# Six small edits around the first output projection: a norm in other banks, the rotation's sum on GpSimd, splits and pair sums of the last head, casts and a lora norm

## The chip, the cores and the metric

The kernel runs on one core of a Trainium2 chip. Its engines are TensorE (PE, matrix products; PEld is its weight load), VectorE (DVE), ScalarE (ACT), GpSimd (POOL) and SyncE (SP), which issues every DMA. The metric is the device time of one launch in microseconds (us), the median of several runs. Times of the trace count from the start of the profiled span.

## The reference

Two encoder layers over 1024 tokens of width 1024, in float32. With `mod` from a conditioning vector `c`, each layer computes

```python
h = rmsnorm(x, norm_g) * (1 + scale) + shift
y = mixer(h)                       # layer 0: differential attention, layer 1: latent attention
x = x + gate * y                   # and a last rmsnorm after layer 1
```

Layer 0 projects `h` to queries, keys, values and a gate `z`, rotates queries and keys (rope), and has eight heads, each with two score maps of head size 64: `p = softmax(s1) - lam * softmax(s2)`, `o = p @ v`, an rmsnorm of `o` per head, `o * silu(z)`, and the output projection `o @ w_out0`. Layer 1 projects to a query latent of 384 and a key/value latent of 256 columns, each with an rmsnorm, expands them per head, and ends with `(o * silu(z)) @ w_out1`.

## The kernel before

**Split products.** A float32 product is computed by three matmuls of a rounded format: each operand is split into a high part (an ACT cast, `S.copy`) and a low part (raw minus high, on DVE or GpSimd), and `mm3` (lines 181 to 184) sums high x high, high x low and low x high in a PSUM bank. An operand is ready when its load has landed, ACT has cast it and the subtraction is done.

**Order.** The code is traced in program order, and a planner then orders each engine's instructions by its own estimate of when they are ready. Every engine, and SP's queue of DMA issues, runs its instructions strictly in that order. The code pins the order in places: `in_turn` (193) and `tc.keep_in_program_order` put an instruction behind the one traced before it on its engine, `tc.issue_after(ins)` and `behind("S")`, `behind("V")` (189) behind a given one, here the newest marked instruction of ACT or DVE. `mk.clear()` ends that in the projection. `side` is a queue of small jobs, of which each step of the projections' stream (`Stream.step`, 305) and each attention tile takes one: a tick.

**Heads of layer 0.** `attn0` (1002) takes a head in eight tiles of 128 queries. A tile (`q_tile`, 834) has two score maps in PSUM (L844, four matmuls each), of each the maximum on DVE (L397) and the exponential on ACT (L399), and the combined `e` on DVE (L852). `transpose_p` (375) transposes `e` through the only `tr` bank (L380), ACT casts it to `pth` (L382), DVE makes `ptl` (L383), and `pv` multiplies by the values. Between these, PE takes steps of the next head's projections. When half a strip of keys or queries is done, `rope` (312) copies it to `rp_raw` on ACT, four DMAs swap its rows into `rp_sw`, GpSimd multiplies by cosines (L324) and, three ticks later, by sines (L329); DVE adds the two (L333) in the job that stands seven ticks after the copy, and that job also stacks the result: two ACT casts (L341, L349), two GpSimd subtractions (L343, L351) and, for queries, four DMAs (L354, L355). Head 0 uses DVE for the cosines.

**The last head.** No projections are left for it. `extra0(i)` (1259) is called after each tile i = 0 to 7, and at three points of `run_tails` as 8, 9, 10. It fetches operands of the output projection (`fa`, `fw`), splits them (`both`), and takes `PRE0[i]` steps of `Pre7` (1201), each one `mm3` of products 0 and 1.

**The output projection** computes the 2 x 2 blocks of `o @ w_out` by seven products of four head pairs each (`Seven`, 1134; `fetch`, `split_a`, `split_w`, `mm`). Sums of heads (`combine`, 1115) are GpSimd operations. The last half head is still unfinished then: `tail0` sums its squares (`ssq`, L922), `tail_b` spreads the reciprocal norm over the partitions with four small products (`finish`, 876; L899, L900, `rb`) and scales `o` (L901); four DVE operations (L1332 to L1335) make its sums, which the third product needs as its fourth operand. PSUM has four `y` and two `tr` banks here; `ssq`, `rb` and half of the second product (`oz`) share the two `tr` banks, and `Y[0]`, `Y[1]` are unused until the third product. Products are added to `x` by `add0` (L1376); a kept part of the first product by `add_p1` (L1373) on GpSimd.

**Layer 1's start.** `group0` normalizes four row tiles (`norm_x`, 446, L454 on DVE or L452 on ACT) and transposes them (`h_chunk`, L465) while the seventh product runs; the first weight strips are loaded and split there (`strip1`, L227, L228). `lora` (1601) sums the squares of the latents over two or three strips on DVE (L1615), and sums that over partitions by four one-column products (L1620), at the step `NORM_AT` of the next half strip.

## Time and profile before

| what | value |
|---|---|
| runs | 1428.61, 1430.06, 1431.25 us; median 1430.06 |
| the profiled execution | 1430.7 us, of which the span of instructions is 1428.9 |
| PE, PEld | 1380.7 and 1149.6 us busy |
| DVE, ACT, POOL | 970.2, 737.0 and 720.0 us busy |
| DMA | 231.52 MB, mean 162 GB/s |
| mean granted clock of PE | 0.990 |

The heads of layer 0 run from about 148 to 704 us, its output projection to about 787, layer 1 from there. In rows of groups, the columns are line, engine, operation, output<-inputs, shape, count, then busy time in us and mean duration in ns, then the idle time of the engine before them and what ended it. In rows of a timeline: start and duration in us, line, operation, count of merged records; in square brackets the idle time before it and what ended that. A float32 matmul of 128 or one column leaves two records.

### The profile page before, as it was taken

The numbers are of one execution on the slowest core, as the hardware profiler recorded it, in microseconds if no ns is written. First come the engines' busy times: TensorE is split into PE (matmuls) and PEld (weight loads), VectorE is DVE, ScalarE is ACT, GpSimd is POOL, SyncE is SP. The second block draws the span as 40 slices with busy tenths as digits, with TensorE's granted clock in tenths as the row PEclk, the third lists the DMA queues.
The fourth block names the chain that finished last, engine by engine and source line by source line (L and its number), as shares of the span: only waits on it lengthen the run. The fifth ranks groups of instructions, "written<-read, shape, count | busy, mean of one in ns | idle before, by whom it ended". The sixth has DMA issues, their size and how long they took to land. (4 is left out here: it accounts for less than half of the span.)

```text
span 1428.9 us, 20757 instructions
## 1 busy us (share of the span) xinstructions
PE 1380.7 (97%) x7318; PEld 1149.6 (80%) x7318; DVE 970.2 (68%) x1383; ACT 737.0 (52%) x1325; POOL 720.0 (50%) x561
## 2 busy tenths in 40 slices
PE   8999999999999999999889999999999999999997
PEld 6777788888878788887767887787888888888886
DVE  8665778877777778677587876545666555555685
ACT  5523465656565556566536543335454454555554
POOL 5425264648585767564784233642131255653783
PEclk9999999999999999999999999999999999999999
DMA  9786634343443444424654136389444355566363
GB/s 345 245 243 196 191 103 131 89 143 104 147 141 113 136 127 121 148 79 166 206 185 155 45 90 215 121 283 257 145 132 119 103 165 190 180 212 210 132 252 118
DMA packets 149065, 231.52 MB, mean 162 GB/s; under 512 B 20577, under 2 KB 57569, under 8 KB 148962
## 3 DMA queue, kind: packets, MB, share of 16 engines
q1 hardware_dynamic: 148962, 230.21, 51.3%
q8 instruction: 57, 0.93, 0.3%
q14 instruction: 46, 0.38, 0.1%
HBM read 144.74 MB, written 61.81 MB: 145 GB/s over the span
## 5 line engine op out<-in xcount | busy, mean ns | idle before, releaser
L382 ACT CAST pth<-tr 128x512 fp32r<-128x512 f32 x256 | 150.4, 588 | 275.9 <-PE tr L380 272.2
L397 DVE TENSOR_REDUCE nm<-s 128x1 f32<-128x1024 f32 x192 | 233.7, 1218 | 67.2 <-PE s L844 55.3
L383 DVE TENSOR_TENSOR ptl<-tr,pth 128x512 fp32r<-128x512 f32 x256 | 176.0, 688 | 137.4 <-ACT pth L382 136.7
L228 POOL TENSOR_TENSOR wl<-wraw,wh 128x512 fp32r<-128x512 f32 (+2 forms) x79 | 104.7, 1327 | 203.8 <-ACT wh L227 190.7
L399 ACT ACTIVATE e<-s,nm 128x1024 f32<-128x1024 f32 x128 | 143.7, 1123 | 35.4 <-DVE nm L397 31.8
L380 PE MATMUL tr<-ident,e 128*128 128x128 f32 x1024 | 155.5, 274 | 5.4 <-DVE ptl L383 4.4
L380 PEld LDWEIGHTS tr<-ident,e 128*128 128x128 f32 x1024 | 120.2, 140 | 48.9 <-DVE ptl L383 25.1
L182 PE MATMUL acc<-h0h,wh 128*128 128x512 f32 x360 | 150.3, 418 | 1.8 <-DVE sl_w L926 0.9
L182 PE MATMUL pv<-pth,vt 128*128 128x256 f32 x512 | 147.4, 288 | 0.7 <-ACT pth L382 0.7
L183 PE MATMUL pv<-ptl,vt 128*128 128x256 f32 x512 | 145.8, 285 | 0.0
L184 PE MATMUL pv<-pth,vt 128*128 128x256 f32 x512 | 144.5, 282 | 0.0
L184 PE MATMUL acc<-h0h,wl 128*128 128x512 f32 x360 | 143.1, 397 | 0.6 <-POOL wl L228 0.6
L183 PE MATMUL acc<-h0l,wh 128*128 128x512 f32 x360 | 141.9, 394 | 0.0
L182 PEld LDWEIGHTS pv<-pth,vt 128*128 128x128 f32 x512 | 97.4, 190 | 3.7 <-ACT pth L382 0.9
L183 PEld LDWEIGHTS pv<-ptl,vt 128*128 128x128 f32 x512 | 97.6, 191 | 2.9
L184 PEld LDWEIGHTS pv<-pth,vt 128*128 128x128 f32 x512 | 97.6, 191 | 0.1
L324 POOL TENSOR_TENSOR rp_r<-rp_raw,cosT 128x512 f32<-128x512 f32 x38 | 50.2, 1322 | 93.0 <-ACT rp_raw L321 37.9
L329 POOL TENSOR_TENSOR rp_sw<-rp_sw,sinT 128x512 f32<-128x512 f32 x42 | 56.8, 1351 | 71.1 <-DMA rp_sw<-rp_raw 71.0
L1167 POOL TENSOR_TENSOR wol<-wol,woh 128x512 fp32r<-128x512 f32 x56 | 82.0, 1489 | 20.5 <-ACT woh L1166 20.5
L844 PE MATMUL s<-ks,qa 128*128 128x512 f32 x256 | 82.9, 405 | 4.3 <-DVE e L852 2.4
L852 DVE SCALAR_TENSOR_TENSOR e<-s,z,e 128x1024 f32<-128x1024 f32 x64 | 82.1, 1283 | 2.1
L184 PEld LDWEIGHTS acc<-h0h,wl 128*128 128x128 f32 x360 | 67.6, 188 | 16.3 <-POOL wl L228 1.1
(406 smaller groups left out, 3491.8 us busy)
## 6 DMA issues: line engine op xcount, KB each, us to landing
ada<-in_ada_ss SPq DMA_DIRECT2D x32, 512.0 KB, 5.4
wraw<-in_w_s SPq DMA_DIRECT2D x64, 256.0 KB, 2.8
vS<-v_hl SPq DMA_DIRECT2D x32, 512.0 KB, 6.0
vt<-vS SPq DMA_DIRECT2D x32, 512.0 KB, 4.1
wol<-tS SPq DMA_DIRECT2D x56, 256.0 KB, 4.8
tS<-ob SPq DMA_DIRECT2D x48, 256.0 KB, 2.0
rp_sw<-rp_raw SPq DMA_DIRECT2D x168, 64.0 KB, 2.0
bc_s<-bc_d SPq DMA_DIRECT2D x34, 256.0 KB, 3.9
```

The source lines that it names most:

```text
L182: PE.matmul(psum, ah, bh, start=first, stop=False, skip_group_check=skip)
L183: PE.matmul(psum, ah, bl, start=False, stop=False, skip_group_check=skip)
L184: mm3.last = PE.matmul(psum, al, bh, start=False, stop=last, skip_group_check=skip).ins
L228: sub = (V if pair_of else G).tensor_sub(l_[:, :n], raw[:, :n], f32v(h_[:, :n]))
L380: PE.transpose(tr[:, j, :], p[:, kt * P : (kt + 1) * P], ident)
L382: mk["S"] = S.copy(pth[kh][:, :, dst], tr).ins
L383: mk["V"] = V.tensor_sub(ptl[kh][:, :, dst], tr, f32v(pth[kh][:, :, dst])).ins
L397: mk["V"] = V.reduce_max(nm, s_ps, axis=AX.X, negate=True).ins
L399: mk["S"] = S.activation(e, s_ps, AF.Exp, bias=nm, scale=1.0, accum_out=zs).ins
L844: PE.matmul(s_ps[:, kc * HF : (kc + 1) * HF], src[:, c, ql], KS[h][kc][:, c, :], start=fst, stop=not fst)
L852: combined.append(V.scalar_tensor_tensor(out=e0, in0=e1, scalar=z1[:, 0:1], in1=e0, op0=ALU.mult, op1=ALU.add).ins)
L1167: sub = eng.tensor_sub(lo, raw, f32v(hi))
```

## The change

- **Norm in free banks.** `ssq` and `rb` of the last half head go to `Y[0]` and `Y[1]`; the four `L899` products go from DVE to ACT.
- **Rotation.** For heads 1 to 7 of layer 0 GpSimd adds right behind its product with the sines; the stack follows two ticks later than before.
- **Last head.** The splits stand one or two steps earlier, the loads of product 1 and of the last pair too, and the pair's sums (`combine`) move from the tail to steps 8 and 9. `PRE0` is spread anew. Layer 0's operand loads, while the heads run, keep their program order on SP, and the steps of `Pre7` stand behind the newest transpose on PE.
- **Kept product.** `add_p1` stands behind the newest GpSimd split.
- **Layer 1's start.** Two of the first group's four row tiles are scaled on ACT; the casts of the first two strips move behind, from one point of the sixth and seventh product to a later one.
- **Lora.** The last strip's square isn't added on DVE: the norm's one-column products sum two tiles instead. `NORM_AT` is 5.

```diff
 V1_AT = (3, 2)
-NORM_AT = 4
-PRE0 = (0, 0, 0, 0, 1, 1, 2, 2, 2, 3, 3)
+NORM_AT = 5
+PRE0 = (0, 0, 0, 0, 1, 2, 2, 2, 2, 2, 3)
 PRE1 = (0, 0, 0, 0, 0, 0, 0, 1, 1, 1, 1)
...
-    def rope(rp, acc, half, scale, eng=G):
+    def rope(rp, acc, half, scale, eng=G, add=V):
...
             in_turn(G.tensor_mul(sw, sw, sinT[:, cs]))
+            if add is G:
+                in_turn(G.tensor_add(r, r, sw))
...
         def fin():
-            with behind("V"):
-                V.tensor_add(r, r, sw)
+            if add is not G:
+                with behind("V"):
+                    V.tensor_add(r, r, sw)
             return r
...
             kt = kh * 4 + j
-            PE.transpose(tr[:, j, :], p[:, kt * P : (kt + 1) * P], ident)
+            transpose_p.last = PE.transpose(tr[:, j, :], p[:, kt * P : (kt + 1) * P], ident).ins
         dst = slice(t * P, (t + 1) * P)
...
         def f(acc, half):
-            rot, fin = rope(wp, acc, half, 1.0, G if h else V)
+            rot, fin = rope(wp, acc, half, 1.0, *[G if h else V] * 2)
...
                 t = a0a.tile([P, 2, HF], F32R, name="ks", tag="ks", bufs=4)
-                stack_k(t, fin())
+                stack_k(t, r.pop() if r else fin())
                 KS.setdefault(h, [None, None])[half] = t
...
-            side.add(*[None] * ROT, rot, *[None] * (DEF - 1 - ROT), g)
+            r = []
+            sum_ = [lambda: r.append(fin()), None] if h else []
+            side.add(*[None] * ROT, rot, *[None] * (DEF - 1 - ROT), *sum_, g)
         return f
...
         def f(acc, half):
-            rot, fin = rope(wp, acc, half, SC0, G if h else V)
+            rot, fin = rope(wp, acc, half, SC0, *[G if h else V] * 2)
...
                 qb = a0a.tile([P, 2, HF], F32R, name="qb", tag="qs", bufs=4)
-                stack_q(qa, qb, fin())
+                stack_q(qa, qb, r.pop() if r else fin())
                 QS.setdefault(h, [None, None])[half] = qa, qb
...
-            side.add(*[None] * ROT, rot, *[None] * (DEF - 1 - ROT), g)
+            r = []
+            sum_ = [lambda: r.append(fin()), None] if h else []
+            side.add(*[None] * ROT, rot, *[None] * (DEF - 1 - ROT), *sum_, g)
         return f
...
             return
-        rb = bank("z" if l else "tr", "rb", [P, HF])
+        rb = bank("z", "rb") if l else Y[1]
         for j in range(4):
             js = slice(j * P, (j + 1) * P)
-            if l:
-                S.mul(dgs[:, js], ident, y[:, j : j + 1])
-            else:
-                V.tensor_scalar(dgs[:, js], ident, y[:, j : j + 1], None, op0=ALU.mult)
+            S.mul(dgs[:, js], ident, y[:, j : j + 1])
             PE.matmul(rb[:, js], ones, dgs[:, js], start=True, stop=True)
...
-    ssq_at = []
+    ssq_at, Y = [], []
...
         def rest():
-            pt = bank("tr", "ssq", [P, HF]) if dst is not None else ssq_at[0] if ssq_at else bank("acc", "ssq")
+            pt = Y[0] if dst is not None else ssq_at[0] if ssq_at else bank("acc", "ssq")
             for j in range(4):
...
         def load(self, home, src):
-            self.last = SP.dma_start(f32v(home[1]), src).ins
+            ins = SP.dma_start(f32v(home[1]), src)
+            self.last = ins.ins
+            if mk and not self.l:
+                tc.keep_in_program_order(ins)
             return *home, f32v(home[1])
...
                 in_turn(sub)
+                self.sub = sub.ins
...
                 ssq_at.append(self.accs[1])
-            self.sv.mm(n, self.accs[i], h, i, start=True)
+            with tc.issue_after(transpose_p.last):
+                self.sv.mm(n, self.accs[i], h, i, start=True)
             self.n += 1
...
             fw(0, 3)
-            SP.dma_start(k0["11"], oF[0][3, 0])
-        if 3 <= i <= 6:
-            both(0, i - 3)
-        if 4 <= i <= 6:
-            fw(1, i - 4)
-            fa(1, i - 4)
+            tc.keep_in_program_order(SP.dma_start(k0["11"], oF[0][3, 0]))
+        for n, h in ((), (), (), ((0, 0),), ((0, 1), (0, 2)), ((0, 3), (1, 0)), ((1, 1),), ((1, 2),), (), (), ())[i]:
+            both(n, h)
+        if i == 4:
+            for h in range(2):
+                fw(1, h)
+                fa(1, h)
+        if i == 5:
+            fw(1, 2)
+            fa(1, 2)
+            fw(1, 3)
         if i == 6:
-            SP.dma_start(k0["21"], oF[0][3, 1])
+            tc.keep_in_program_order(SP.dma_start(k0["21"], oF[0][3, 1]))
             k0["pair"] = [pw.tile([P, HF], F32, name="ob", tag="ob", bufs=4) for _ in range(4)]
-        if i == 7:
-            fw(1, 3)
             for t, (hh, half) in zip(k0["pair"], ((2, 0), (6, 0), (2, 1), (6, 1))):
-                SP.dma_start(t, oF[0][hh, half])
-        if 7 <= i <= 9:
-            both(1, i - 7)
-        if i == 10:
+                tc.keep_in_program_order(SP.dma_start(t, oF[0][hh, half]))
+        if i == 8:
             sv.split_w(1, 3)
...
                 sv.kept[n][2] = t
+            k0["sum"] = combine(*k0["pair"])
+        if i > 7:
+            next(k0["sum"], None)
         for _ in range(PRE0[i]):
...
         for i, t in enumerate(p1s):
-            G.tensor_add(xf[rows + i][:, halves[f]], xf[rows + i][:, halves[f]], t)
+            with tc.issue_after(sv0.sub):
+                G.tensor_add(xf[rows + i][:, halves[f]], xf[rows + i][:, halves[f]], t)
...
         V.tensor_add(ssa[gi], ssa[gi], ssb[gi])
-        norm_x(ssa[gi], fulls, (2, 3) if gi else ())
+        norm_x(ssa[gi], fulls, (2, 3) if gi else (1, 3))
...
     Z = pre0.accs
-    Y = [bank("y", "oy") for _ in range(4)]
+    Y += [bank("y", "oy") for _ in range(4)]
     for h in range(4):
...
             tail_b = tail0()
-            for _ in combine(*k0["pair"]):
-                pass
     for i in range(2):
...
                 with tc.issue_after(w6):
-                    w4.append(strip1(0))
+                    raws = fetch_strip([A["w_s1"][0, f] for f in range(2)], [4, 4])
+            if i == 0 and n == 6:
+                w4.append(split_strip(raws))
             if i == 1 and n == 6:
-                w4.append(strip1(1, h1p))
+                raws = fetch_strip([A["w_s1"][1, f] for f in range(2)], [4, 4])
+            if i == 3 and n == 6:
+                w4.append(split_strip(raws, h1p))
         if n == 3:
...
         craw = [[None, None] for _ in range(n)]
-        sums = [None, None]
+        sums, last = [None, None], [None, None]
+
         def put(i, half, acc):
...
                 lm["S"] = S.activation(s2, acc, AF.Square).ins
-                lm["V"] = V.tensor_add(sums[half], sums[half], s2).ins
+                if i < n - 1:
+                    lm["V"] = V.tensor_add(sums[half], sums[half], s2).ins
+                else:
+                    last[half] = s2
...
             for j in range(4):
-                PE.matmul(pt[:, 0, j : j + 1], sums[half][:, j * P : (j + 1) * P], ones[:, 0:1], start=True, stop=True)
+                for t in (sums[half], last[half]):
+                    PE.matmul(pt[:, 0, j : j + 1], t[:, j * P : (j + 1) * P], ones[:, 0:1], start=t is sums[half], stop=t is last[half])
             wv = sm.tile([P, 4], F32, name="c_w")
...
```

## The prediction

> **What bounds the kernel now.** I read the page's busy times first, then the waits of TensorE (PE; columns: total, times, longest), then busy time by stretch (columns: length, then PE, its weight loads, DVE, ACT and POOL, with instructions in brackets, granted clock, DMA share, GB/s).
>
> ```profile
> PE 1380.7 (97%) x7318; PEld 1149.6 (80%) x7318; DVE 970.2 (68%) x1383; ACT 737.0 (52%) x1325; POOL 720.0 (50%) x561
> ```
> ```profile
> PE rb L900 <- DVE x L1376: 6.6, 1, 6.6
> ...
> PE oy L183 <- POOL wol L1167: 3.6, 3, 2.3
> ```
> ```profile
> 199.00:634.00 435.00, 429.61 (x2385) 360.91 (x2384) 324.10 (x451) 253.34 (x445) 273.30 (x223) 1.00 0.41 123
> ...
> 656.00:694.00 38.00, 30.74 (x179) 24.14 (x178) 27.53 (x42) 26.85 (x50) 20.75 (x18) 1.00 0.61 195
> ...
> 714.00:725.00 11.00, 4.53 (x16) 3.97 (x17) 8.93 (x12) 3.07 (x6) 8.55 (x6) 0.69 0.57 210
> ```
>
> PE sets the time: it is 97% busy, so what the change does to another engine counts only where it ends a wait of PE, or adds one. PE is idle for 1428.9 - 1380.7 = 48.2 us in all, and the change reaches five places of that: A, the wait for `rb` (6.6 us); B, the last head of layer 0 (656 to 694: 38.00 - 30.74 = 7.3); C, the first norm of layer 1; D, one lora norm; E, heads 1 to 7 of layer 0 (435.00 - 429.61 = 5.4, and one wait behind that window). Behind some of these gaps the granted clock is low (0.69 from 714 to 725), so a gap can cost more than its length.
>
> **A: `rb` in a free bank.** PE's timeline, DVE's beside it, and the groups that give prices:
>
> ```profile
> 720.47 2.07 PE L900 MATMUL rb<-sq,ones 128*128 128x128 f32 x8 [6.62 <-DVE x L1376]
> 722.20 0.77 PE L182 MATMUL oz<-woh,oah 128*128 128x512 f32 x1
> ...
> 724.47 0.39 PE L184 MATMUL oz<-woh,oal 128*128 128x512 f32 x1
> 724.70 0.39 PE L182 MATMUL oy<-woh,oah 128*128 128x512 f32 x1
> ```
> ```profile
> 708.38 5.03 DVE L899 TENSOR_SCALAR sq<-ident,rq_y 128x128 f32<-128x128 f32 x4 [1.18 <-POOL rq_y L930]
> ...
> 719.75 0.67 DVE L1376 TENSOR_TENSOR x<-x,oz 128x512 f32<-128x512 f32 x1
> ...
> 722.58 0.69 DVE L901 TENSOR_TENSOR o<-o,rb 128x512 f32<-128x512 f32 x1 [1.08 <-PE rb L900]
> ...
> 730.61 0.68 DVE L1167 TENSOR_TENSOR oal<-k,oah 128x512 fp32r<-128x512 f32 x1
> ```
> ```profile
> L900 PE MATMUL rb<-dg,ones 128*128 128x128 f32 x8 | 1.1, 274 | 0.0
> ```
> ```profile
> L452 ACT ACTIVATE x<-x,rq_y 128x1024 f32<-128x1024 f32 x2 | 2.2, 1144 | 1.6 <-POOL rq_y L169 1.6
> ```
> ```profile
> 714.60 0.62 ACT L1166 CAST oah<-ob 128x512 fp32r<-128x512 f32 x1 [8.71 <-POOL ob L1119]
> ```
>
> `rb` waits not for its operand (the `L899` products end at 713.4) but for its bank: the `tr` bank is held until `L1376` has read a tile of the second product, 719.75 + 0.67 = 720.4. In `Y[1]` no one is in the way. That gives 6.6, plus 1.0 (`rb` takes 2.07 here, 1.1 for the same eight records in layer 1), plus 1.1 of slow clock (five starts from 722.20 to 724.47 take 2.27; at the 0.23 between the last two rows 1.14): 8.7 at most.
>
> The four `L899` products go to ACT. 128 columns have no row there; they lie between nothing and the 1.14 of 1024 columns, so at most 4.6 together. From 708.4 that ends by 713.0, before PE comes to `rb` at 720.47 - 6.62 = 713.85, on an ACT that is idle for 8.71 then: no cost by either bound. If ACT were not idle, `rb` would wait for what is left.
>
> Late next is the third product. `Y[1]` is its second bank, so it waits for `L901`; and its fourth operand comes down the chain from `L901` to the split at 730.61, from 722.58 to 731.3, 8.7 us. PE's room is six matmuls and then 36 of the third product, 42 x 0.23 = 9.7. That is one microsecond of slack, on a DVE that does the adds of two products meanwhile; behind a waiting `L901` on DVE stand just those adds, which free banks for the fourth product. I take **7.0** (2 to 8.7). The pair sums, four GpSimd operations at 708 to 716 now, leave this stretch, which helps. The adds of the kept product move behind the weight splits on GpSimd's queue; the banks that wait for them are wanted one product (48 x 0.23 = 11 us) later: nothing, or what those splits exceed 11 us by.
>
> **B: the last head.** PE's timeline, and one row of GpSimd's:
>
> ```profile
> 680.59 0.50 PE L183 MATMUL oy<-wol,oah 128*128 128x512 f32 x1 [2.28 <-POOL wol L1167]
> ...
> 690.79 0.66 PE L380 MATMUL tr<-ident,e 128*128 128x128 f32 x4 [1.68 <-DVE ptl L383]
> ...
> 693.70 0.70 PE L182 MATMUL oy<-woh,oah 128*128 128x512 f32 x1
> ...
> 697.16 0.39 PE L184 MATMUL oy<-woh,oal 128*128 128x512 f32 x1
> ```
> ```profile
> 674.09 1.28 POOL L915 TENSOR_TENSOR o<-o,gz 128x512 f32<-128x512 f32 x1 [5.84 <-ACT o L909]
> ```
>
> At stake are the 7.3 idle and the slow stretch behind (eight starts in 3.46 against 8 x 0.23 = 1.8, so 1.6): 8.9. The waits for `wol` (3.6) come from splitting an operand in the very step that uses it. After the change every split stands at least a step ahead of its use, and its load a step ahead of the split. From step 4 on there are 13 splits and four pair sums, the same as before, only earlier: 17 x 1.28 = 22 us on a GpSimd that is busy 20.75 of 38 now and idle for 5.84 before 674.09; what doesn't fit makes `wol` late again (R2). The fetches and the loads of the pair are pinned on SP's queue, each behind what was traced before it (a finished head's store, its two broadcasts); a late one holds all SP behind it, and a step of some 6.5 us covers a landing of 4 to 5 only if the queue stands free. The wait at 690.79 is for the single `tr` bank: `pth`, then `ptl`. There ACT has fewer casts in the way, and the partial products, pinned behind the transposes, fill 1.4 us. In steps 4 and 5, though, ACT gets four casts instead of two, 1.2 us more per step that can stand ahead of an exponential or a `pth`. I take **5.5** (0 to 8.9).
>
> **C: the first norm of layer 1.** PE, then DVE:
>
> ```profile
> 768.68 0.39 PE L465 MATMUL trh<-ident,x 128*128 128x128 f32 x1 [1.34 <-DVE x L454]
> 768.77 0.74 PE L182 MATMUL oy<-woh,oah 128*128 128x512 f32 x1
> ...
> 772.26 0.39 PE L184 MATMUL oy<-woh,oal 128*128 128x512 f32 x1
> ```
> ```profile
> 761.77 6.85 DVE L454 TENSOR_SCALAR x<-x,rq_y 128x1024 f32<-128x1024 f32 x4 [1.19 <-POOL rq_y L169]
> ```
>
> Four scalings on DVE, 1.71 each, end at 768.6. With two on ACT (1.14 each) DVE is through at 761.77 + 3.4 = 765.2 and ACT at about 764.1, before PE asks for the last one (768.68 - 1.34 = 767.3). At stake: this 1.3, a wait of 0.6 on the tile before it, and 1.7 of clock (eight starts in 3.49): 3.6. The casts of two weight strips (`L227`) move behind, out of ACT's way, under the 11 us of the seventh product; if that cover fails, the first strip is late by one split, 1.3. I take **2.8** (1.5 to 3.6).
>
> **D: the lora norms.** PE's timeline and the group:
>
> ```profile
> 860.02 1.02 PE L1620 MATMUL cps<-ones,csum 128*128 128x1 f32 x8 [2.11 <-DVE csum L1615]
> 860.91 0.72 PE L182 MATMUL acc<-h1h,wh 128*128 128x512 f32 x1
> ...
> 864.40 0.40 PE L184 MATMUL acc<-h1h,wl 128*128 128x512 f32 x1
> ```
> ```profile
> L1620 PE MATMUL cps<-ones,csum 128*128 128x1 f32 x32 | 3.9, 242 | 2.1 <-DVE csum L1615 2.1
> ```
>
> The last square no longer passes DVE, and the norm stands a step (0.7 us) later, so ACT's square is in time: one wait of 2.1 goes, with 1.7 of slow clock behind it. For that all four norms sum two tiles: 32 more records at (1.02 - 0.25) / 7 = 0.11, so 3.5 us of PE. Sum **+0.2** (-1.5 to 0.3).
>
> The Trainium skill ("TensorE: Matmul & The Clock Gate", section "Why this matters for your kernels") says that the clock falls for idle gaps of more than about 3 us. By it the gap of 2.1 would have cost no clock, D would be -1.4 and the whole 1415. The row disagrees: starts are 0.43 apart right behind that gap.
>
> **E: the rotation's sum on GpSimd.** Groups, then rows of DVE, PE and SP:
>
> ```profile
> L333 DVE TENSOR_TENSOR rp_r<-rp_r,rp_sw 128x512 f32<-128x512 f32 x42 | 41.1, 979 | 17.9 <-POOL rp_sw L329 17.7
> L329 POOL TENSOR_TENSOR rp_sw<-rp_sw,sinT 128x512 f32<-128x512 f32 x42 | 56.8, 1351 | 71.1 <-DMA rp_sw<-rp_raw 71.0
> ```
> ```profile
> 560.50 1.23 DVE L397 TENSOR_REDUCE nm<-s 128x1 f32<-128x1024 f32 x1 [1.41 <-PE s L844]
> ...
> 630.77 1.23 DVE L397 TENSOR_REDUCE nm<-s 128x1 f32<-128x1024 f32 x1 [1.21 <-PE s L844]
> ...
> 635.07 2.00 DVE L333 TENSOR_TENSOR rp_r<-rp_r,rp_sw 128x512 f32<-128x512 f32 x1 [1.02 <-POOL rp_sw L329]
> ```
> ```profile
> 491.18 0.70 PE L844 MATMUL s<-ks,qb 128*128 128x512 f32 x2 [0.32 <-DMA qb<-qb]
> ...
> 638.92 0.70 PE L844 MATMUL s<-ks,qa 128*128 128x512 f32 x2 [1.30 <-DVE e L852]
> ```
> ```profile
> 554.19 0.46 SPq L355 DMA_DIRECT2D qb<-qb  x1
> ...
> 626.40 0.46 SPq L355 DMA_DIRECT2D qb<-qb  x1
> ```
> ```profile
> qb<-qb SPq DMA_DIRECT2D x32, 128.0 KB, 2.3
> ```
>
> 28 of the 42 sums leave DVE (28 x 0.98 = 27 us); GpSimd gets 28 x 1.35 = 38, some 32 of it in the window where it is busy for 273 of 435: from 63 to 70%, no bound. On DVE a sum of 2.0, as at 635.07 (and 1.0 of waiting for its operand), puts off the maximum or `e` behind it, and PE waits (638.92). All idle time of these heads is 5.4 + 1.3 = 6.7. On GpSimd the sum waits for nothing but the product just ahead of it; behind it stand the scale of a finished head, weight splits and the stacks, each 1.35 later. Against the gain: the casts come two ticks later. The head from 560.50 to 630.77 has 48 steps and 8 tiles in 70.3 us, 1.25 per tick, so 2.5 us, less the 1 to 2 for which the casts now wait on DVE. `qb` has little room: at 491.18 PE waits for it already; issued at 626.40 it lands at 628.7, and the scores that use it start about 629.7 (four matmuls before 630.77); 2.9 us are left in the head before (554.19 to 560.50). I take **1.5** (-4 to 6.7).
>
> **Sum.** 7.0 + 5.5 + 2.8 + 0.2 + 1.5 = 17.0. Against this execution's 1430.7 (a span of 1428.9 and 1.8 around it; the median, 1430.06, is 0.6 lower): **1413.7 us**.
>
> **Rivals.** R1: A's wait moves to the third product, for `L901` or the split that ends at 731.3. One microsecond of slack speaks for it; that the pair sums and `L899` leave the stretch speaks against. A gives 2: 1418.7. R2: the last head becomes bound by its casts and splits. DVE is busy 27.53 of 38 there and ACT 26.85, so neither is full, but they take turns. B gives 0: 1419.2.
>
> R3, slower: GpSimd makes `qb` late in every head. The three tightest heads have 0, 1.0 and 2.9 of slack; a delay d costs these three 3d - 3.9. With E's gain gone this meets the 15.5 of A to D at d = 6.5; at 7.5 (the two ticks and four GpSimd operations more ahead of the stacks) it costs 18.6: 1433.8. Against it: GpSimd is idle for 37% of the window, and the sum is ready before the casts' tick. The Trainium skill speaks for R3 ("GPSIMD Engine Reference", section "Engine selection"): it wants two-input elementwise work on VectorE, GpSimd being about twice as slow at it.
>
> R4: the instructions come out in another order than the edits intend, and the gaps only change places: 1430.
>
> **How the numbers follow.** Forecast 0.52 (its own range 1408 to 1418), R1 0.15, R2 0.14, both 0.05 (1424), R4 0.05, R3 0.09. All upper bounds together would give 1402.5, hardly to be had. The range, 1404 to 1425, leaves out R3, R4 and a little. A measurement can tell about 0.2% (2.9 us) from no change: faster 0.86, same 0.05, slower 0.09.
>
> **What would show it.** A: no wait ahead of `rb`, and a clock near 1 from 714 to 725; a wait of the third product for `L901` or `oal<-k` is R1. B: no wait for `wol`; waits of `tr` or `s` for ACT are R2. C: no wait of `trh`. D: 64 `cps` records, none waiting. E: `L333` x14 on DVE. Waits of `s` for `qb` beyond 3 us in all would be R3's way, and a slower kernel by any other chain would make the prediction wrong in its premise.

## The result, and the profile after

The changed kernel takes **1430.95 us** (1428.3 to 1434.6), the kernel before 1431.97 in the same runs: a ratio of 0.9995, 95% interval 0.9985 to 1.0004. The forecast was 1413.7; nothing measurable came of the 17 us. The profiled execution took 1428.8 us, with a span of 1427.0.

Three views of the changed kernel: the page's busy times, the waits of PE (total, times, longest), and busy time by the same stretches as before. Its lines are numbered up to 14 higher: the scores are L851, the first norm's transposes L468, `rb` L904 (in a `y` bank, so named `oy`).

```profile
PE 1382.6 (97%) x7350; PEld 1154.4 (81%) x7350; DVE 937.9 (66%) x1345; ACT 737.0 (52%) x1331; POOL 751.1 (53%) x589
```
```profile
PE s L851 <- DMA qa<-qa: 6.9, 4, 2.9
...
PE s L851 <- DVE e L859: 3.2, 3, 2.4
PE trh L468 <- DVE x L457: 2.9, 2, 2.0
PE oy L183 <- POOL wol L1174: 2.5, 1, 2.5
PE trh L468 <- DVE h L477: 2.0, 2, 1.8
```
```profile
199.00:634.00 435.00, 426.75 (x2375) 361.25 (x2374) 297.04 (x425) 252.14 (x447) 300.33 (x247) 1.00 0.42 122
656.00:694.00 38.00, 31.31 (x172) 25.44 (x170) 26.89 (x41) 25.22 (x46) 21.91 (x19) 0.91 0.52 165
714.00:725.00 11.00, 11.00 (x54) 9.27 (x53) 10.93 (x12) 5.82 (x12) 11.00 (x8) 1.00 1.03 391
```

What A and D were to end has gone: nothing waits for `rb`, nothing ahead of `cps`, and the stretch from 714 to 725 is full at a clock of 1.00 (it was 4.53 of 11 at 0.69). Of the waits for `wol`, 2.5 of 3.6 are left. The waits for DVE at layer 1's first transposes are 4.9 (`x` and `h`), where the kernel before has 2.0 (`x`). New are 6.9 for `qa` and one wait of 2.4 for `e`. And the last head runs at a clock of 0.91 instead of 1.00.

Marks that both traces have (the first maximum of a head, L400 or L397; the last matmul of `pv`; the first and last transpose of layer 1's first norm) split the difference of the spans. Two of the changed kernel's marks:

```profile
635.37 1.22 DVE L400 TENSOR_REDUCE nm<-s 128x1 f32<-128x1024 f32 x1 [2.40 <-PE s L851]
```
```profile
703.14 0.28 PE L184 MATMUL pv<-pth,vt 128*128 128x256 f32 x1
```

| stretch | before, us | after, us | change | forecast |
|---|---|---|---|---|
| start to head 0's first maximum | 147.89 | 148.44 | +0.6 | |
| to head 7's first maximum (E) | 482.88 | 486.93 | +4.1 | -1.5 |
| to the last `pv` (B) | 70.94 | 67.77 | -3.2 | -5.5 |
| to layer 1's first transpose (A) | 64.30 | 58.44 | -5.9 | -7.0 |
| to the last transpose there (C) | 40.46 | 43.30 | +2.8 | -2.8 |
| to the end (D) | 622.40 | 622.08 | -0.3 | -0.2 |
| span | 1428.87 | 1426.96 | -1.9 | -17.0 |

So the stretches of E and C have the wrong sign, and those of B and A pay less than forecast. A stretch isn't yet its part, though: the experiments show below that part of B's comes from E. These are single executions, and the runs of either kernel spread over 5 to 6 us.

**Theory 1**, formed from this: each edit takes its own wait away, but puts an instruction that itself waits into a strictly ordered queue ahead of what PE wants next. **Rival 2**: from the last head to layer 1 a chain on DVE, ACT and GpSimd sets the end, and PE's waits only change places.

### The profile page after: what moved, and what is told of

It is laid out like the page before. It is cut to its first block, busy times and chain, and to the rows that moved or that the text cites. A ratio compares the mean times of both kernels' runs of the same rounds, so it can differ in the third digit from the quotient of the medians.

```text
span 1427.0 us, 20754 instructions
## 1 busy us (share of the span) xinstructions
PE 1382.6 (97%) x7350; PEld 1154.4 (81%) x7350; DVE 937.9 (66%) x1345; ACT 737.0 (52%) x1331; POOL 751.1 (53%) x589
## 5 line engine op out<-in xcount | busy, mean ns | idle before, releaser
L400 DVE TENSOR_REDUCE nm<-s 128x1 f32<-128x1024 f32 x192 | 233.9, 1219 | 98.5 <-PE s L851 86.7
L851 PE MATMUL s<-ks,qa 128*128 128x512 f32 x256 | 84.2, 410 | 11.6 <-DMA qa<-qa 6.9
L851 PE MATMUL s<-ks,qb 128*128 128x512 f32 x256 | 81.2, 398 | 0.5 <-DMA qb<-qb 0.5
```

What stands on the lines that cost most here:

```text
L400: mk["V"] = V.reduce_max(nm, s_ps, axis=AX.X, negate=True).ins
L851: PE.matmul(s_ps[:, kc * HF : (kc + 1) * HF], src[:, c, ql], KS[h][kc][:, c, :], start=fst, stop=not fst)
```

## The experiments

Each ratio is to the kernel before, with its 95% interval.

### E: the rotation

Taken out of the changed kernel, taken in without its two ticks, the ticks without the engine, and by itself:

```diff
# e3_no_rotation (from after)
-rope(wp, acc, half, 1.0, *[G if h else V] * 2)
+rope(wp, acc, half, 1.0, G if h else V)
-sum_ = [lambda: r.append(fin()), None] if h else []
+sum_ = []
# ... the same for the queries, with SC0
# e2_no_ticks (from after): only the second pair of lines
# e9_ticks_only (from before)
-side.add(*[None] * ROT, rot, *[None] * (DEF - 1 - ROT), g)
+side.add(*[None] * ROT, rot, *[None] * ((DEF + 1 if h else DEF - 1) - ROT), g)
# e17_rotation_only (from before): e9's line, and the sum on GpSimd
```

> The changed kernel with the rotation as before (sum on DVE, stack at the old tick). Theory: the 7.4 us of waits for qa and qb go and the old 6.7 us of these heads come back, so within 2 us of the changed kernel, or up to 2 faster. Rival (the heads don't matter, the loss is in the projection alone): the time stays the changed kernel's within 1 us and waits of the heads don't change.

Measured 1430.59, 0.9998 [0.9986, 1.0011]: as the changed kernel. Its trace is another, though. The waits for `qa` are gone, and the heads take 483.0 us instead of 486.9. But the last head takes 2.0 more and the first norm 2.9 more, with this wait:

```profile
PE trh L468 <- DVE h L477: 4.0, 1, 4.0
```

What the heads gain without E is lost behind them here.

> The changed kernel, but the stack follows the rotation at the old place in the queue of small jobs, without the two added ticks; the sum stays on GpSimd. If the two ticks make qa and qb late: the waits of s for qa and qb fall from 7.4 to under 3 us in all, and the time is 3 to 5 us under the changed kernel. If GpSimd's own lateness (its sum ends 9 to 13 us after the raw copy, against 6 to 11 on DVE) makes them late: the waits stay above 5, the time is within 2 us of the changed kernel.

Measured 1442.59, 1.0073 [1.0054, 1.0092]: 10 us slower, which neither expectation has. ACT's and PE's timeline of that run show why:

```profile
212.02 0.62 ACT L352 CAST qa<-rp_r 64x512 fp32r<-64x512 f32 x1 [4.85 <-POOL rp_r L331]
212.55 1.11 ACT L402 ACTIVATE e<-s,nm 128x1024 f32<-128x1024 f32 x1
```
```profile
218.19 0.66 PE L383 MATMUL tr<-ident,e 128*128 128x128 f32 x4 [2.26 <-DVE ptl L386]
```

The stack's cast stands on ACT 4.85 us for the sum, with an exponential behind it, and PE is short of `e` a tile later. So the place of the casts matters, and with it the two ticks:

> Kernel before with one edit: in heads 1 to 7 of layer 0 the job that sums the rotation and stacks it stands two ticks later; the sum stays on DVE. Theory 1 (the rotation's edit takes the waits that the DVE sums caused, some 6.5 in the heads, and pays the same again in waits of the scores for qa and qb, because the stack stands two ticks later): here nothing is gained and the waits for qa and qb of some 7 us appear: 1437.5. Rival 2 (qa and qb are late because the sum on GpSimd itself and the queue behind it are slower, not because of the ticks): no new waits for qa and qb, 1431.

Measured **1427.19, 0.9981 [0.9971, 0.9992]**: 3 us faster, and both theories wrong. The waits for `qa` are there, but only 1.9 us. Groups of 199 to 656 us, the last column being the engine's idle time ahead of them; before, the run without ticks, the ticks alone, and the changed kernel:

```profile
L333 DVE TENSOR_TENSOR rp_r<-rp_r,rp_sw 128x512 f32<-128x512 f32 x25 | 27.4, 1096 | 9.3 <-POOL rp_sw L329 9.1
...
L349 ACT CAST qa<-rp_r 64x512 fp32r<-64x512 f32 x13 | 8.1, 621 | 13.7 <-DVE rp_r L333 13.7
```
```profile
L352 ACT CAST qa<-rp_r 64x512 fp32r<-64x512 f32 x13 | 8.1, 620 | 20.1 <-POOL rp_r L331 20.1
```
```profile
L333 DVE TENSOR_TENSOR rp_r<-rp_r,rp_sw 128x512 f32<-128x512 f32 x25 | 26.0, 1040 | 2.7 <-POOL rp_sw L329 2.7
...
L349 ACT CAST qa<-rp_r 64x512 fp32r<-64x512 f32 x14 | 8.7, 620 | 4.0 <-DVE rp_r L333 4.0
```
```profile
L352 ACT CAST qa<-rp_r 64x512 fp32r<-64x512 f32 x14 | 8.7, 620 | 2.2 <-POOL rp_r L331 2.2
```

Before, DVE stood 9.3 us for the rotated product and ACT 13.7 for the sum, each with PE's next feed queued behind. Two ticks take most of both away, on whichever engine the sum is. That leaves the move itself:

> Kernel before with the rotation's edit alone: the sum on GpSimd, the stack two ticks later. The run with the two ticks and the sum left on DVE is at 0.998 of before. Theory 3 (the two ticks give the gain, and the move to GpSimd takes it back, since each sum takes longer there and stands in one queue with the stack's subtractions): waits for qa and qb of 6 to 8, and 1430 to 1431. Rival (the engine does not matter): as with the ticks only, waits for qa and qb below 3, 1427.5.

Measured 1433.38, 1.0022 [1.0010, 1.0034]. Its waits for `qa`, and those of the ticks alone:

```profile
PE s L847 <- DMA qa<-qa: 6.4, 4, 2.6
```
```profile
PE s L844 <- DMA qa<-qa: 1.9, 2, 1.3
```

The same ticks with the sum on GpSimd make the kernel slower than before, by 0.2%, and some 6 us slower than the ticks alone. The waits are as theory 3 of its expectation has them; the time is 2 to 3 us above its 1430 to 1431. Which link behind the sum makes `qa` late wasn't separated: one sum takes 1.32 us on GpSimd and 1.04 on DVE, and GpSimd has the rotation's products and the stack's subtractions in the same queue.

The traces of all runs bear it out. From head 0's to head 7's first maximum it takes 481.8 to 483.5 us in the nine with the sum on DVE at the old tick, 481.0 to 483.1 in the five with it on DVE at the later tick, and 486.4 to 491.0 in the five with it on GpSimd at the later tick. The ticks shorten the last head too, with none of B's edits there: from 70.9 us to 69.1 in e9 and 68.6 in e17. Why they do wasn't looked into.

### B: the last head

ACT, PE and GpSimd of the changed kernel:

```profile
659.94 0.62 ACT L1173 CAST woh<-wol 128x512 fp32r<-128x512 f32 x1 [0.80 <-DMA wol<-tS]
660.47 1.08 ACT L402 ACTIVATE s<-s,nm 128x1024 f32<-128x1024 f32 x1
```
```profile
663.55 1.22 PE L851 MATMUL s<-ks,qa 128*128 128x512 f32 x2 [2.40 <-DVE e L859]
...
683.55 0.50 PE L183 MATMUL oy<-wol,oah 128*128 128x512 f32 x1 [2.52 <-POOL wol L1174]
```
```profile
679.77 1.01 POOL L169 TENSOR_TENSOR rq_y<-sl_w,mhalf 128x4 f32<-128x4 f32 x1 [2.04 <-DVE sl_w L932]
...
681.01 1.26 POOL L1174 TENSOR_TENSOR oal<-k,oah 128x512 fp32r<-128x512 f32 x1
682.23 1.26 POOL L1174 TENSOR_TENSOR wol<-wol,woh 128x512 fp32r<-128x512 f32 x1
```

The first weight cast waits for its load with the second map's exponential behind it. The load's place on SP is pinned behind a small broadcast:

```profile
655.46 0.32 SPq L408 DMA_DIRECT2D bc_d<-rq_y  x1
655.84 0.42 SPq L1154 DMA_DIRECT2D wol<-tS  x1
```

And the splits of product 0's fourth operand stand behind a four-column operation of the norm that waits 2.04 for DVE. Are the pins the fault?

```diff
# e6_no_pins (from after): the three tc.keep_in_program_order(...) around layer 0's loads removed
```

> The changed kernel without the pins on SP's queue: the planner places the loads of the output projection's operands again. Theory 1: the wait of 2.4 at 663.6 (scores for e: ACT's exponential stands behind a weight cast that waits for a load issued behind a store and two broadcasts) and the slow clock behind it go; the wait of 2.5 for wol at 683.3, whose splits stand behind a small GpSimd operation that waits for DVE, stays: 1428.5. Rival 2: the stretch from 656 to 694 keeps its length within 1 us, as other waits take the place: 1430.9.

Measured 1432.68, 1.0012 [0.9997, 1.0026]. They are at fault for that wait, which shrinks to 1.5, and the last head takes 66.1 us instead of 67.8. But without them the third product waits 4.7 for `o`, and layer 1's transposes 3.8 for `h`, so nothing is gained. Then A and B (with the kept product) without the rest, and with the norm of C:

> Kernel before with A (norm in free banks), B (last head, with the pins) and the kept product alone: no change to the rotation, the norm of layer 1, the strips or the lora norms. Theory 1: A pays its 6 to 8 as soon as the pair sums are out of the way, B pays 1 to 3, and behind them 4 to 6 of new waits of trh for x give most of it back: 1428.3, and faster than A alone (1431.3). Rival 2: as A alone, 1431.

Measured 1428.80, 0.9983 [0.9969, 0.9997], near theory 1.

> The run with A, B and the kept product, and two of the four scalings of layer 1's first norm on ACT; no change to the rotation, the strips or the lora norms. Theory 1: the waits of trh for x fall from 4 to 6 to about 3 and nothing waits for h: 1426.5, the fastest of all. Rival 2: no faster than the run without the norm's change, 1430 to 1431.

Measured 1428.00, 0.9982 [0.9968, 0.9997], no faster than without the norm's change: the waits for `x` fall from 5.7 to 3.2, but 3.1 for `h` come, where theory 1 has none. The cast waits 2.46 in this run, and PE 4.1 for `e`. The last head takes 72.3 us in e7 and 72.8 in e8, longer than the 70.9 before, and 69.7 in e3, which has all but E. So B's edits by themselves change it by -1.2 to +1.9, and of the 3.2 in the table about 2 are E's ticks. Two repairs, one after the other:

```diff
# e10_early_loads (from e8); Seven.load pins only while sv.pin is True
+            sv.pin = False
             for h in range(2):
                 fw(0, h)
                 fa(0, h)
+            sv.pin = True
# e11_early_splits (from e10)
-((0, 1), (0, 2)), ((0, 3), (1, 0)),
+((0, 1), (0, 2), (0, 3)), ((1, 0),),
```

> The run with A, B, the kept product and the norm on ACT (1428.0), with one edit: the first four loads for the output projection, fetched after the third tile of the last head, are not pinned on SP's queue; all later ones are. Theory 1: they are issued before the small broadcast and land some 5 us earlier, ACT's first weight cast no longer stands waiting in front of the exponential, and PE's wait of 4.1 for e at 664 falls below 1, with the slow matmuls behind it; the wait of 2.5 for wol at 684 stays: 1423.5. Rival 2 (DVE and ACT bound the last head by turns whatever PE waits for): the wait for e shrinks, others grow, and from the first maximum of head 7 to the last product of the values nothing changes by more than 1: 1428.

Measured 1425.38, 0.9963 [0.9948, 0.9978]. The wait for `e` falls to 1.5, not below 1, and that for `wol` stays:

```profile
661.80 0.73 PE L851 MATMUL s<-ks,qa 128*128 128x512 f32 x2 [1.50 <-DVE e L859]
...
681.25 0.50 PE L183 MATMUL oy<-wol,oah 128*128 128x512 f32 x1 [2.52 <-POOL wol L1175]
```

> As the run with the early loads, and the split of the fourth operand of product 0 stands one step earlier too, ahead of the small GpSimd operation of the last head's norm. Theory 1: the wait of 2.5 for wol at 684 goes as well, and the time is 2 us below the run with the early loads alone: 1421.5. Rival 2: four casts and six GpSimd subtractions in one step put off an exponential or another split instead, and the time is not below the run with the early loads.

Measured **1422.77, 0.9954 [0.9937, 0.9971]**: no wait for `wol` is left, and a new one of 2.5 stands at the last transposes, which theory 1 didn't have. From head 7's first maximum to the last `pv` it takes 67.9 us, where e10 takes 68.7 and e8 72.8. Two small causes in queue order were worth some 5 us together, and rival 2 falls for this stretch; what the second adds to the first isn't clear of noise.

### A: the norm of the last half head

```diff
# e1_only_a (from before): rb in Y[1], ssq in Y[0], the four products on ACT
```

> The kernel before with the free banks alone: ssq and rb in Y[0] and Y[1], the four L899 products on ACT. Theory (each edit's gain is real, but E, B and C each put a waiting instruction into a strictly ordered queue): the rb wait of 6.6 and its slow clock go and about 2 come back at the first norm of layer 1, so some 6 us faster than before. Rival (a chain over DVE, ACT and GpSimd bounds the stretch from the projection to layer 1, whatever PE waits for): the gain reappears as waits of trh, at most 2 us faster.

Measured 1431.32, 0.9998 [0.9987, 1.0008]: nothing. The theory's 6 us don't come, and they don't reappear at the transposes either, as the rival had it. PE no longer waits for `rb` but for what comes next, as R1 said:

```profile
715.51 0.50 PE L183 MATMUL oy<-wol,oah 128*128 128x512 f32 x1 [1.35 <-POOL wol L1164]
...
720.00 0.79 PE L182 MATMUL oy<-woh,oah 128*128 128x512 f32 x1 [3.77 <-DVE o L898]
```

Then A taken out of the repaired kernel (below):

> The repaired kernel with A taken back: the last half head's squares and norm in the two tr banks, the four products with the identity on DVE. Theory 1: A alone gave nothing, because behind it the third product waited for the pair sums' splits and for o; with the pair sums moved, A is worth 5 to 7: 1425 to 1427 here, with the wait of 6 or more for rb back. Rival 2: A stays worth nothing, since the chain from o's scaling to the third product's fourth operand is as late: 1420.

Measured 1422.36, 0.9940 [0.9925, 0.9955]: as fast as with A (1423.06), so theory 1 misses. With both in the `tr` banks again nothing waits for `rb`: sharing the bank costs nothing as long as it is read in time. DVE's four products there, and GpSimd, which is idle beside them:

```profile
701.20 0.88 DVE L906 TENSOR_SCALAR sq<-ident,rq_y 128x128 f32<-128x128 f32 x4 [1.41 <-POOL rq_y L937]
```
```profile
705.95 5.95 POOL L1178 TENSOR_TENSOR wol<-wol,woh 128x512 fp32r<-128x512 f32 x4 [4.78 <-ACT woh L1177]
```

The same four take 5.03 in the kernel before, where GpSimd runs four pair sums and two adds of the kept product from 708 to 716, this add among them:

```profile
709.54 1.29 POOL L1373 TENSOR_TENSOR x<-x,p 128x512 f32<-128x512 f32 x1
```

Is that the cause?

```diff
# e16_pair_sums_only (from before): the pair's loads to step 6, combine to steps 8 and 9
# e18_products_on_act (from before)
-            if l:
-                S.mul(...)
-            else:
-                V.tensor_scalar(...)
+            S.mul(dgs[:, js], ident, y[:, j : j + 1])
```

> Kernel before with one edit: the pair's loads one step and its four GpSimd sums from the tail to steps 8 and 9 of the last head; banks, products with the identity on DVE, weight splits and pins as before. In kernel before the four products L899 take 5.03 on DVE while GpSimd works on the pair's sums from 708.3 to 716; in the repaired kernel without A the same four take 0.88 beside an idle GpSimd, and rb doesn't wait. Theory 3 (the wait of 6.6 for rb comes from DVE instructions that GpSimd's hold up, and the pair sums' move is what A was credited with): L899 takes below 1.5 in all, the wait for rb is gone or below 1, and the last product of the values to layer 1's first transpose takes 58 to 60 instead of 64.3: 1425 to 1427. Rival (the prediction's: the bank): rb still waits for L1376 some 6, and the time stays at 1430 to 1431.

Measured 1437.53, 1.0054 [1.0041, 1.0067]. DVE's products and two waits of PE:

```profile
716.96 5.03 DVE L899 TENSOR_SCALAR sq<-ident,rq_y 128x128 f32<-128x128 f32 x4 [1.19 <-POOL rq_y L930]
```
```profile
PE oy L183 <- POOL wol L1167: 7.7, 5, 3.4
PE rb L900 <- DVE x L1380: 5.5, 1, 5.5
```

Not the test that it was meant to be: GpSimd wasn't idle. It now did weight splits at 717, the products took 5.03 again, and the sums pushed the last head's splits back (7.7 for `wol`). Moved without the earlier splits, the pair sums only cost.

> Kernel before with half of A: the four products with the identity of the last half head on ACT; the banks stay. Theory 3 (rb waits because GpSimd's weight splits and pair sums hold DVE's four products for 5.03, and the adds that free the bank stand behind them): without these four on DVE the adds come up to 5 earlier, and the wait for rb falls from 6.6 to between 1 and 3; as with A alone, most of that comes back behind it, so 1429 to 1431. Rival (the bank alone: the second product's place in the order sets when the tr bank is read, whatever DVE does before): the wait for rb stays above 5.

Measured 1432.72, 1.0011 [0.9998, 1.0024]. Theory 3 misses: without the products on DVE, the wait for `rb` stays, and DVE idles where they were:

```profile
PE rb L897 <- DVE x L1373: 6.7, 1, 6.7
```
```profile
713.86 0.69 DVE L1373 TENSOR_TENSOR x<-x,oy 128x512 f32<-128x512 f32 x1 [3.67 <-POOL x L1370]
716.36 1.28 DVE L1373 TENSOR_TENSOR x<-x,oy 128x512 f32<-128x512 f32 x2 [1.82 <-POOL x L1370]
```

DVE's adds wait for GpSimd's adds of the kept product (L1370, L1373 in before), which stand between the pair sums, and then DVE waits 0.60 for the cast of a pair sum. The add that frees the bank stands behind them. So in e18 the wait is GpSimd's queue, two links behind the name in the bracket; in the kernel before, DVE has no gap there, as the slow products fill it, and the add comes just as late. So, by these traces, two routes lead from GpSimd to the bank, and taking one away gives nothing.

What cures it isn't separated. All runs in which this stretch is short (58 to 59 us) have B's earlier splits, the pair sums in the last head and the kept product behind the splits. The pair sums alone don't do it (e16: 63.4 us). The run without the pins (e6) has all of these edits, and A, but there GpSimd's weight splits come late again, the kept product stands behind them, and DVE waits:

```profile
720.55 1.93 DVE L1388 TENSOR_TENSOR x<-x,oy 128x512 f32<-128x512 f32 x3 [6.21 <-POOL x L1385]
```

The scaling of `o` stands behind that, and the stretch takes 62.9.

### C: the first norm and the strips

```diff
# e4_no_norm_strip (from after): norm_x(..., (2, 3) if gi else ()), and strip1(0), strip1(1) at their old points
# e5_strip_back (from after): only the strips
```

> The changed kernel with the first norm wholly on DVE and the two strips loaded and split where they were. Theory (the casts stand in ACT's queue ahead of h_h while their load is late): the wait of trh for DVE h (2.0) goes; that for DVE x grows to some 4 from 2.9; the time is about as the changed kernel or 2 faster. Rival (a chain bounds this stretch): waits of trh in all stay at 4.9 or grow, and the time is the changed kernel's or up to 2 slower.

Measured 1429.29, 0.9988 [0.9975, 1.0002].

> The changed kernel with the casts and subtractions of the first two strips of layer 1 back at their old points; the norm stays on ACT and DVE. Theory 1 (each edit takes its own wait away, but puts an instruction that itself waits into a queue of strict order ahead of PE's feed): in the changed kernel ACT's high part of h stands behind a strip cast that waits 1.3 for its load, and PE's wait of 1.8 for h at 776.5 comes from that; here that wait is below 0.4, the two waits of trh for x (1.95 and 0.9) stay, and the time is 1429.2. Rival 2 (from the last head to layer 1 a chain on DVE and ACT sets the end, and PE's waits only change places): the 1.8 comes back as waits of trh for x, above 4 in all, and the time stays at 1430.9.

Measured 1429.66, 0.9989 [0.9976, 1.0001]. Neither differs from the changed kernel by more than the intervals. Waits in the first and the second:

```profile
PE trh L468 <- DVE x L457: 5.7, 4, 2.0
```
```profile
PE trh L468 <- DVE x L457: 3.2, 2, 2.0
...
PE trh L468 <- DVE h L477: 1.2, 2, 0.9
```

The norm on two engines takes 2.5 of the waits for `x`, and most comes back as waits for `h`: the stretch from the first to the last transpose gets 0.5 shorter (42.9 to 42.4), as from e7 to e8 (43.6 to 43.1). What is left in the changed kernel is in DVE's and ACT's timelines:

```profile
752.90 1.87 DVE L1390 TENSOR_TENSOR x<-x,oz 128x512 f32<-128x512 f32 x3
758.20 0.16 DVE L1398 TENSOR_TENSOR ss<-ss,ss 128x4 f32<-128x4 f32 x1 [3.43 <-ACT tjunk L1481]
...
759.76 3.43 DVE L457 TENSOR_SCALAR x<-x,rq_y 128x1024 f32<-128x1024 f32 x2 [1.20 <-POOL rq_y L169]
```
```profile
753.67 0.63 ACT L1394 ACTIVATE tjunk<-x 128x512 bf16<-128x512 f32 x1 [1.99 <-DVE x L1390]
...
757.45 0.63 ACT L1481 ACTIVATE tjunk<-x 128x512 bf16<-128x512 f32 x1
```
```profile
761.58 0.77 PE L468 MATMUL trh<-ident,x 128*128 128x128 f32 x2 [1.95 <-DVE x L457]
```

Three adds come in one bunch, ACT does six squares in a row behind them, and the sum of squares waits 3.43 for ACT. PE gets there 6 us earlier than before, because of the tail, and meets this chain: here rival 2 holds, as read from the trace; no run took the chain away. The other traces fit. In the six runs whose stretch to the first transpose takes 63.4 to 64.3 us (the kernel before, e1, e9, e16, e17, e18), the next one takes 40.2 to 40.8; in the thirteen where it takes 58.1 to 58.8, the next takes 42.3 to 47.2. So some 2 us or more of what the tail gains are lost right behind it, with C's edits or without (e7: 43.6). The strips add one wait more, where ACT's `h_h` stands behind a cast that waits for its load:

```profile
774.34 0.62 ACT L227 CAST wh<-wraw 128x512 fp32r<-128x512 f32 x1 [1.31 <-DMA wraw<-in_w_s]
774.87 0.77 ACT L473 ACTIVATE h_h<-trh,modb,moda 128x512 fp32r<-128x512 f32 x1
```

### The parts put together

```diff
# e12_repaired: e11, and the rotation's sum on DVE two ticks later
-            sum_ = []
+            sum_ = [None, None] if h else []
# e14_repaired_lora: e12 with the lora norms (D) as changed
# e13_change_repaired: e14 with the strips (C) as changed, that is the whole change with three repairs
```

> The run with the early loads and splits (1422.8: A, B, the kept product and the norm on ACT), and the rotation's sum on DVE in a job two ticks later, as in the run with the ticks only (3 us faster than before). Theory 1: the two gains are in different stretches and add up: DVE's waits for the rotated rows stay below 4 us, and the time is 1419.8. Rival 2: the stack that comes two ticks later meets the last head's loads and broadcasts on SP's queue, and less than half of the 3 us is left: 1421.5 or more.

Measured 1423.06 (1417.8 to 1425.7), 0.9937 [0.9916, 0.9959]. By its median this is rival 2, no faster than e11; the two gains (e9 and e11) add up only by the ratios (0.9981 x 0.9954 = 0.9935), and the intervals of e11 and e12 overlap. The stretches speak for theory 1: heads and last head are 1.1 and 2.7 us shorter than in e11, but the next is 1.0 longer.

> The repaired kernel (early loads and splits, sum on DVE two ticks later, strips at their old points) with the lora norms as changed (D). The prediction's own price: 3.5 of PE for 32 more one-column records against 3.8 of waits and slow clock, so the same time as without D, 1419.8 by theory 1, within 1.5. Rival: the second lora norm's three sums wait anyway, and D costs the 3.5 in full: 1423.

Measured **1421.40 (1419.4 to 1422.9), 0.9934 [0.9917, 0.9951]**: D is worth nothing that shows, as the prediction has it.

> The whole changed kernel, parts A to E, strips and lora norms among them, with three repairs: the first four loads not pinned, the split of the fourth operand of product 0 one step earlier, and the rotation's sum on DVE at the later tick. Theory 1: the 17 us that were missing are 7 to 8 in the last head, 5 to 7 in the rotation's engine, 1 to 2 in the strips; with the first two repaired: 1421. Rival 2: the strips and lora norms cost more than in single traces, 1423 or more.

Measured 1424.12 (1424.1 to 1424.8), 0.9954 [0.9941, 0.9968]: rival 2. Its interval doesn't reach the changed kernel's, so the repairs are worth some 6 us there (0.9995 - 0.9954). It differs from e14 by the strips alone, and the times of their five runs each don't overlap, though the intervals of the ratios just do. Its waits for `h`, and e14's:

```profile
PE trh L468 <- DVE h L477: 5.4, 1, 5.4
```
```profile
PE trh L468 <- DVE h L477: 2.7, 3, 1.5
```

So the strips cost some 2 to 3 us. The fastest version, e14, is 9 us below the kernel before.

## Why the prediction was wrong

- **E, the step with the wrong sign.** "On DVE a sum of 2.0 ... and 1.0 of waiting for its operand" was read as the engine's fault, and "the casts come two ticks later" was booked as a cost. It is the other way round: the two ticks gain some 3 us, the engine loses some 6 (e9, e17). "From 63 to 70%, no bound" weighed a share of busy time where the lateness of each sum counts. R3 had GpSimd's lateness right, but for `qb` (0.5 us of waits in the changed kernel) where it was `qa` (6.9); by itself the edit costs some 3 us (e17), not 18.6. Nor is GpSimd twice as slow at the sum here: 1.32 us against 1.04.
- **A, near the number for a wrong reason, which is luck.** "`rb` waits ... for its bank ... In `Y[1]` no one is in the way" stopped at the first releaser. The stretch did give 5.9 of the 7.0, but A alone gives 0 (R1, e1), and without A the 6 are there as well (e15). They come with the earlier splits, the pair sums and the kept product's adds, for which the sum books nothing in this stretch; which of the three is needed stays open.
- **B, sized too high.** "After the change every split stands at least a step ahead of its use, and its load a step ahead of the split" is true of the code's steps, not of the queues. A pinned load came late and its cast held an exponential; the split came behind an operation that waits. As they stand, B's edits change the last head by -1.2 to +1.9 us instead of -5.5, and about 2 of the 3.2 measured there are E's ticks. That R2 would be casts in the way was right; that the last head would be bound by them was not: two lines moved gave 5 us (e10, e11).
- **C, the sum's own mistake.** The price of 2.8 took PE's demand at 767.3 from the trace of before, while the gains ahead of it move that demand 6 us forward. The terms are in series: the norm on two engines gives 0.5, and behind a short tail this stretch is some 2 us longer or more in every run. That the statistics of the norm are the chain there is read from the trace, not tested. C's strips, for which the text allows at most 1.3, cost 2 to 3 (e13, e14).
- **D** was right: nothing. Its side sum of 1415 takes the clock term out of D alone, though B and C have such terms too (1.6 and 1.7), behind gaps below 2.3 us.
- **R4** has the number, 1430, and half of the reason: gaps changed places. That the instructions came out in another order than the edits intend isn't shown.
- The premise, that only PE's waits count, held: PE is idle for 44.4 us (1427.0 - 1382.6) instead of 48.2, and busy 1.9 longer. What failed is that a wait was priced by the name in its bracket, and that terms were added which share a chain.

## What to carry to other kernels

Before pricing a wait, follow its releaser's engine two or three instructions back: where the named thing alone was taken away here, the time didn't come, because what had made the releaser late stayed. In a kernel of strict queues, an instruction that waits costs what stands behind it. Here the job placed two ticks later, when its operand was there, gained; the same job on another engine lost. And where one gain brings the bounding engine earlier to the next stage, price that stage anew before adding its term.

## What the runs showed of the hardware

- Beside a busy GpSimd, four DVE products of 128 x 128 took 5.03 us, 1.26 each, which is the length of one GpSimd operation; beside an idle one 0.88 in all (kernel before and e15). The Trainium skill ("SBUF — State Buffer", section "SBUF: two separate sides") says that GpSimd shares a port pair with those DVE instructions that run in a two-port mode or have two SBUF inputs, and that whichever starts first holds it for the whole instruction while the other stands still. These rows agree with it; in which mode the four products ran, no run here shows.
- The clock fell behind short gaps: 0.91 over the last head of the changed kernel (656 to 694 us), whose two longest gaps are 2.40 and 2.52 us, with the two matmuls behind the first taking 1.22 (0.73 behind the 1.50 of e10). The length of the gap alone doesn't decide it: in e10 a gap of 2.52 us at the same place leaves the clock at 1.00 over the same window.
